# Moving the two halves of an output bank together: two half-bank copies and two adds, or one whole-bank copy and two adds across partitions

## The chip, the cores and the metric

The program runs on one core of a Trainium2 chip. The core has a matrix engine (TensorE, PE), a vector engine (VectorE, DVE), a scalar engine (ScalarE, ACT), a general engine (GpSimd, POOL) and a queue engine that issues most transfers (SyncE, SP). Each engine takes its instructions in the order in which they stand in its own queue, and waits on semaphores for the others. SBUF and PSUM are memories of 128 partitions; PSUM has banks of 512 float32 per partition. The metric is the device time of one launch in microseconds; less is better.

## The reference

A two-layer decoder trunk over 1024 tokens of width 1024, 16 heads of 64 in 4 key/value groups. Layer 0 has a native sparse attention (attention A in this document), layer 1 a dilated attention (attention B). Each is followed by an output projection and a SwiGLU feed-forward block. Cut to what matters here:

```python
# layer 0: three branches, gated and summed per head
o = g[..., 0:1] * o_cmp + g[..., 1:2] * o_sel + g[..., 2:3] * o_win
# layer 1: three (window, dilation) groups, merged by their softmax denominators
alpha = jax.nn.softmax(jnp.stack(lses, axis=-1), axis=-1)
o = jnp.einsum('bsgrdi,bsgri->bsgrd', jnp.stack(outs, axis=-1), alpha)
# in every branch: o = softmax(q k^T * scale + bias, masked) v
```

The product of the probabilities with v is what the change touches: how it leaves PSUM.

## The kernel before

Values are float32 throughout. Where a product needs more than one pass of the matrix engine, an operand is split into a rounded high part and the rest: `v` is stored with the high part in columns 0 to 63 and the low part in columns 64 to 127. A product of `v` with probabilities, both parts of `v` at once, therefore gives 128 partitions: partitions 0 to 63 (the lower half) hold the share of the high part and partitions 64 to 127 (the upper half) that of the low part. The two must be added across partitions, once per output bank. That is `evac_o` (L353 to L360).

An output bank `o` (PSUM, 128 x 512) holds the four heads of one group for 128 tokens, 128 columns per head. In `ov` the heads are numbered by c (0, 1) and e (0, 1). Heads with e = 0 go to the lower half of `dst`, heads with e = 1 to the upper half. For each e, `own` is the half that the result is written to and `oth` the other one: ScalarE copies the other half of the bank to the partitions of `own` in the SBUF buffer `ot` (L359), and VectorE adds the bank's own half and the copy (L360). There are two `o` banks (BANKS, L30).

Attention A (L624 to L866) runs over 4 groups g and 8 tiles t of 128 tokens. For each (g, t) come a compressed-block job (`cmp_job`), which opens the bank with L760 and L761, and four `dense_job`s: window branch and selected-block branch, each for two pairs of heads (hp). A job does scores on PE (L790, L791), bias and minimum on VectorE (L793), exponentials on ScalarE (L799), normalising on GpSimd (L803). Its `back` part transposes the probabilities on PE (L328), moves them to SBUF as `th` (ScalarE, L165) and `tl` (VectorE, L166), or by a plain copy `traw` (L332, L340), and multiplies with `v` (L347 to L349). The last `back` of a (g, t) calls `evac_o`, which writes to `oT`.

Attention B (L1560 to L1783) has for each of 4 groups 8 wide jobs per head pair (`wide_job`, dilation groups 1 and 2 together, result to `o12`, whose tokens lie 8 apart) and then 8 near jobs per head pair (`near_job`, dilation group 0, result to `oTb`). Scores, bias (L1641), exponentials (L1646) and the `back` part follow the same pattern. The second head pair of each pair calls `evac_o`. A generator `merge` joins the results of a group (L1702 to L1747). So `evac_o` runs 32 times in A, 32 times for wide and 32 times for near jobs.

`pipelined` puts the `back` part of a job two jobs later. Beyond that the order is not written by hand: the tile framework's scheduler decides, from its own estimate of durations, in which order instructions stand in each engine's queue (`schedule_with_timeline_sim`, L1835). So an edit in `evac_o` can move other instructions too. After each attention comes `out_proj` (L1219), whose first loads are `ow` (L1228, weights) and `xr` (L1237, the residual stream).

Of the kernel before, what the change touches and what calls it, by code (L numbers as in the profile page):

```python
# [10 lines left out]
F32 = mybir.dt.float32  # L11
F32R = mybir.dt.float32r
BF = mybir.dt.bfloat16
AF = mybir.ActivationFunctionType
# [101 lines left out]
def trunk(ctx, tc, I, out):  # L116
    nc = tc.nc
# [235 lines left out]
    def evac_o(p, po, dst):  # L353

        ov = po[:].rearrange("p (c e q) -> p c e q", e=2, q=128)
        tmp = p.tile([128, 2, 128], F32, name="ot", bufs=2)
        for e in range(2):
            own, oth = slice(64 * e, 64 * e + 64), slice(64 - 64 * e, 128 - 64 * e)
            nc.scalar.activation(tmp[own], ov[oth, :, e, :], AF.Copy)  # L359
            nc.vector.tensor_add(dst[own], ov[own, :, e, :], tmp[own])  # L360

    def pipelined(jobs, lag=1):

# [260 lines left out]
    with ExitStack() as c:  # L624
# [139 lines left out]
        def dense_job(g, t, br, hp):  # L764
# [41 lines left out]
            def back():  # L806
                po = po_[g, t]
                for b0 in range(0, nb, 2):
                    bs = range(b0, min(b0 + 2, nb))
                    th, tl = transposed(wk, [P[:, e, b * 128:(b + 1) * 128] for b in bs for e in range(2)],  # L810
                                        (cp_a, cp_v)[hp] if br == 2 and b0 == 2 else None,
                                        whole=br == 2 and hp == 1 and b0 == 0)
                    for i, b in enumerate(bs):
                        last = br == 1 and b == nb - 1
                        cs = slice(i * 256, (i + 1) * 256)
                        o_ = po[:, hp * 256:(hp + 1) * 256]
                        v_ = grp["V", br - 1, g, (k0 + b) // 4][:, (k0 + b) % 4, :]
                        mm_pv(o_, v_, th, tl, cs, False, last)
                if br == 1 and hp == 1:
                    evac_o(wk, po, oT[:, 2 * g:2 * g + 2, tok(t)])  # L820
# [739 lines left out]
    with ExitStack() as c:  # L1560
# [73 lines left out]
        def unit(key, hp, stats, slot, score, bias, n, blocks, dst):  # L1634
# [14 lines left out]
            def back():  # L1649
                if hp == 0:  # L1650
                    po_[key] = bank("o"), None
                po, prev = po_[key]
                nb = len(blocks)
                for b0 in range(0, nb, 2):
                    bs = range(b0, min(b0 + 2, nb))
                    th, tl = transposed(wk, [P[:, e, b * 128:(b + 1) * 128] for b in bs for e in range(2)],
                                        pick(hp, b0, nb), 5, unsplit(key, hp))
                    for i, b in enumerate(bs):
                        cs = slice(i * 256, (i + 1) * 256)
                        o_ = po[:, hp * 256:(hp + 1) * 256]  # L1660
                        with after(prev if b == 0 else None):
                            prev = mm_pv(o_, blocks[b], th, tl, cs, b == 0, b == nb - 1)
                po_[key] = po, prev
                if hp == 1:
                    evac_o(wk, po, dst)
# [173 lines left out]
```

## Time and profile before

| | us |
|---|---|
| median of 3 runs | 2975.21 |
| lowest and highest run | 2972.13, 2981.29 |
| span of the profiled execution, first to last instruction | 2969.9 |

For the profiled execution no time is given beside its span; the median of the runs, which also holds what lies around the span, is 5.3 us above it. The page gives busy time for each engine. For VectorE and ScalarE an instruction's time is what it keeps the engine; on PE the ends of matmuls are modelled and neighbours overlap, so a busy PE is not PE at its peak. The name after the line number is the tile that is written, then what is read. The granted TensorE clock is 0.989 on average and 1.00 in both attentions.

### The profile page before, as it was taken

The page shows a single profiled execution, that of the slowest core. Times are in us where ns is not written, and L with a number is a line of the kernel's source. Part 1 is how long each engine was busy: PE and PEld are TensorE (multiplying, and loading weights), DVE is VectorE, ACT ScalarE, POOL GpSimd, SP SyncE. Part 2 cuts the span into 40 slices and gives each one's busy share as a digit, 9 for nine tenths or more (in the row PEclk, how much of TensorE's full clock was granted, in tenths as well). Part 3 has the DMA queues.
Part 4 walks back from the last instruction along what each step waited for, and adds up shares of the span by engine and source line. Part 5 has one row for each costly group of instructions (what it writes and reads, how often), then busy time and mean ns, then how long its engine had stood idle before and what let it go on. Part 6 is the DMA issues. An engine that isn't in the chain of part 4 may idle for free.

```text
span 2969.9 us, 44462 instructions
## 1 busy us (share of the span) xinstructions
PE 2839.8 (96%) x14734; PEld 2368.8 (80%) x14734; DVE 2398.1 (81%) x4875; ACT 1608.9 (54%) x3614; POOL 1607.7 (54%) x1718
## 2 busy tenths in 40 slices
PE   9999999999999999999999999899989999999997
PEld 8888888887777788788777788788867787887885
DVE  5553988988888888988876676699998888888887
ACT  5432888897553333333454444799965433333334
POOL 3135766764565555555557786444426655556551
PEclk9999999999999999999999999999999999999998
DMA  8678133113222222231224555966340211112112
GB/s 252 209 246 285 46 91 87 54 30 118 68 62 64 73 75 62 62 81 53 86 81 143 160 165 152 288 195 181 101 167 22 68 57 53 57 47 64 54 43 75
DMA packets 277318, 317.58 MB, mean 107 GB/s; under 512 B 19196, under 2 KB 210733, under 8 KB 277088
## 3 DMA queue, kind: packets, MB, share of 16 engines
q1 hardware_dynamic: 255344, 246.50, 27.9%
q0 software_dynamic: 21744, 68.23, 7.1%
q8 instruction: 117, 1.92, 0.3%
q14 instruction: 113, 0.93, 0.1%
HBM read 243.17 MB, written 87.20 MB: 111 GB/s over the span
## 4 chain that ended last, share of the span: by engine, by line
PE 62%; DVE 23%; ACT 6%; issue 4%; POOL 2%; DMA 2%; SPq 1%; DVEq 0%; ACTq 0%; POOLq 0%
PE ux L203 5%; PE ux L204 5%; DVE pl L885 5%; PE ux L205 5%; PE uy L203 4%; PE uy L204 4%; PE uy L205 4%; DVE xr L943 4%; PE dx L204 3%; PE dx L205 3%; PE pt L328 3%; PE dr L203 3%; PE dx L203 3%; PE mm L204 3%; PE mm L203 3%
## 5 line engine op out<-in xcount | busy, mean ns | idle before, releaser
L885 DVE TENSOR_TENSOR pl<-oT,ph 128x512 fp32r<-128x512 f32 x319 | 327.2, 1045 | 42.5 <-ACT ph L884 37.2
L884 ACT ACTIVATE ph<-oT 128x512 fp32r<-128x512 f32 x329 | 198.4, 625 | 206.8 <-PE ux L204 58.9
L328 PE MATMUL pt<-ident,P 128*128 128x128 f32 x1536 | 242.3, 275 | 10.6 <-DVE tl L166 4.9
L885 DVE TENSOR_TENSOR pl<-oTb,ph 128x512 fp32r<-128x512 f32 x233 | 222.3, 979 | 25.2 <-ACT ph L884 25.2
L166 DVE TENSOR_TENSOR tl<-pt,th 128x512 fp32r<-128x512 f32 (+1 forms) x336 | 217.4, 652 | 26.8 <-ACT th L165 25.5
L884 ACT ACTIVATE ph<-oTb 128x512 fp32r<-128x512 f32 x239 | 142.8, 625 | 170.2 <-PE ux L204 52.5
L943 DVE TENSOR_TENSOR xr<-xr,dr 128x512 f32<-128x512 f32 x320 | 204.3, 678 | 29.9 <-PE dr L205 29.9
L204 PE MATMUL dx<-pl,ph 128*128 128x512 f32 x512 | 206.3, 403 | 9.9 <-DVE pl L885 7.3
L803 POOL TENSOR_SCALAR P<-P,sm,gates 128x384 f32<-128x384 f32 (+7 forms) x256 | 182.5, 724 | 45.2 <-DVE sm L801 40.0
L165 ACT ACTIVATE th<-pt 128x512 fp32r<-128x512 f32 (+1 forms) x336 | 185.0, 564 | 37.4 <-PE pt L328 31.6
L205 PE MATMUL dx<-ph,pl 128*128 128x512 f32 x512 | 202.5, 398 | 0.3 <-DVE pl L885 0.3
L328 PEld LDWEIGHTS pt<-ident,P 128*128 128x128 f32 x1536 | 177.7, 141 | 31.4 <-DVE tl L166 5.2
L943 DVE TENSOR_TENSOR xr<-xr,dx 128x512 f32<-128x512 f32 x320 | 199.9, 676 | 2.5 <-PE dx L205 1.8
L203 PE MATMUL dx<-ph 128*128 128x512 f32 x512 | 165.6, 403 | 15.9 <-DVE nss L1016 7.9
L799 ACT ACTIVATE P<-P,m 128x384 f32<-128x384 f32 (+7 forms) x256 | 170.6, 669 | 9.0 <-DVE m L797 7.2
L1269 POOL TENSOR_TENSOR oT<-oT,gffn 128x512 f32<-128x512 f32 x92 | 107.7, 1177 | 118.8 <-DMA oT<-in_ffn_w_up_dram 96.5
L348 PE MATMUL o<-th,V 128*128 128x256 f32 x572 | 158.7, 297 | 4.5 <-DVE o L360 1.7
L349 PE MATMUL o<-tl,V 128*128 128x256 f32 x572 | 158.2, 299 | 4.7 <-DVE tl L166 1.7
L1269 POOL TENSOR_TENSOR oTb<-oTb,gffn 128x512 f32<-128x512 f32 x92 | 106.5, 1167 | 87.9 <-DMA oTb<-in_ffn_w_up_dram 79.8
L341 POOL TENSOR_SCALAR th<-traw 128x256 fp32r<-128x256 f32 x112 | 95.4, 852 | 98.2 <-ACT traw L340 33.1
L1646 ACT ACTIVATE P<-P,st 128x384 f32<-128x384 f32 (+2 forms) x256 | 139.9, 548 | 6.3 <-DVE st L1641 5.0
L203 PEld LDWEIGHTS dx<-ph 128*128 128x128 f32 x512 | 97.8, 191 | 45.4 <-ACT nss L1015 8.7
(629 smaller groups left out, 9487.8 us busy)
## 6 DMA issues: line engine op xcount, KB each, us to landing
qB<-xr POOLq DMA_DIRECT2D x96, 256.0 KB, 4.6
oT<-in_ffn_w_up_dram SPq DMA_DIRECT2D x92, 256.0 KB, 3.0
oTb<-in_ffn_w_up_dram SPq DMA_DIRECT2D x92, 256.0 KB, 3.0
Q<-qB SPq DMA_DIRECT2D x40, 512.0 KB, 6.4
wd<-in_ffn_w_down_dram SPq DMA_DIRECT2D x66, 256.0 KB, 2.6
oT<-in_b_w_q_dram SPq DMA_DIRECT2D x48, 256.0 KB, 3.4
K<-kBs SPq DMA_DIRECT2D x40, 256.0 KB, 9.6
wraw<-in_a_w_in_dram SPq DMA_DIRECT2D x18, 512.0 KB, 7.1
```

The lines of the kernel that those rows point to most:

```text
L165: prev = nc.scalar.activation(H_, src, AF.Copy)
L166: rest = (eng or nc.vector).tensor_sub(L_, src, f32(H_))
L203: nc.tensor.matmul(ps, lh, rh, start=first, stop=False, skip_group_check=bool(shared))
L204: nc.tensor.matmul(ps, lh, rl, start=False, stop=False, skip_group_check=bool(shared))
L205: return nc.tensor.matmul(ps, ll, rh, start=False, stop=last, skip_group_check=bool(shared))
L328: nc.tensor.transpose(ps[:, i * 128:(i + 1) * 128], b, ident)
L799: nc.scalar.activation(P[:, e, :n], P[:, e, :n], AF.Exp, bias=mm[:, e:e + 1], scale=-1.0, accum_out=sm[:, e:e + 1])
L803: nc.gpsimd.tensor_scalar(P[:, e, :n], P[:, e, :n], sm[:, e:e + 1], gt(g, t, br, 2 * hp + e, 1), op0=OP.mult, op1=OP.mult)
L884: nc.scalar.activation(h, src, AF.Copy)
L885: (eng or nc.vector).tensor_sub(l, src, f32(h))
L943: nc.vector.tensor_add(xs, xs, banks[t])
L1269: nc.gpsimd.tensor_mul(v, v, gains[:, k:k + 4].unsqueeze(2).to_broadcast([128, 4, 128]))
```

## The change

The buffer `ot` gets the size of a whole bank (128 x 2 x 2 x 128 in place of 128 x 2 x 128) and one place instead of two, so it takes the same memory. ScalarE copies the whole bank to it once, every partition to itself. VectorE then does its two adds: for each e, the own half of the bank, read from PSUM, and the other half of the copy, read from SBUF at the other partitions. Until now both inputs and the output of an add lay on the same partitions.

```diff
     def evac_o(p, po, dst):
 
         ov = po[:].rearrange("p (c e q) -> p c e q", e=2, q=128)
-        tmp = p.tile([128, 2, 128], F32, name="ot", bufs=2)
+        tmp = p.tile([128, 2, 2, 128], F32, name="ot", bufs=1)
+        nc.scalar.copy(tmp[:].rearrange("p c e q -> p (c e q)"), po)
         for e in range(2):
             own, oth = slice(64 * e, 64 * e + 64), slice(64 - 64 * e, 128 - 64 * e)
-            nc.scalar.activation(tmp[own], ov[oth, :, e, :], AF.Copy)
-            nc.vector.tensor_add(dst[own], ov[own, :, e, :], tmp[own])
+            nc.vector.tensor_add(dst[own], ov[own, :, e, :], tmp[oth, :, e, :])
```

ScalarE has 192 half copies (64 x 256) before and 96 copies (128 x 512) after; every other engine has the same instructions, in another order inside the two attentions. Outside of them only the start of the output projection after A, with its loads, has changed order.

First place: VectorE in attention B, wide jobs of the second group, near their end. Before (`ot` is the buffer, `o_21047` the result `o12`, `st_21045` the row statistics, `T_...` the bias; what a row waits for is in brackets):

```order
L166 TENSOR_TENSOR tl<-pt,th 128x512 [waits Activation_49]
L360 TENSOR_TENSOR o_21047<-o,ot 64x256 [waits Activation_49]
L1641 ISA P,st_21045<-s,T_20684 128x384 [waits PE_49]
L1641 ISA st_21045 128x1
L360 TENSOR_TENSOR o_21047<-o,ot 64x256 [waits Activation_49]
L1641 ISA P,st_21045<-s,T_20687 128x384 [waits PE_49]
L1641 ISA st_21045 128x1
L166 TENSOR_TENSOR tl<-pt,th 128x512 [waits Activation_49]
```

Each of the two adds of a bank waits for ScalarE, and other work stands between them. The same place on VectorE after the change (`o_21000` is `o12`, `st_20998` the statistics):

```order
L166 TENSOR_TENSOR tl<-pt,th 128x512 [waits Activation_49]
L360 TENSOR_TENSOR o_21000<-o,ot 64x256 [waits Activation_49]
L360 TENSOR_TENSOR o_21000<-o,ot 64x256
L1641 ISA P,st_20998<-s,T_20643 128x384 [waits PE_49]
L1641 ISA st_20998 128x1
L1641 ISA P,st_20998<-s,T_20646 128x384 [waits PE_49]
L1641 ISA st_20998 128x1
L166 TENSOR_TENSOR tl<-pt,th 128x512 [waits Activation_49]
```

The two adds stand next to each other and only the first waits; this is so for all 96 banks.

Second place: ScalarE in attention B, near jobs of the second group. Before:

```order
L359 ACTIVATE ot<-o 64x256 [waits PE_49,Activation_49]
L165 ACTIVATE th<-pt 128x512 [waits PE_49]
L359 ACTIVATE ot<-o 64x256 [waits DVE_49]
L1646 ACTIVATE P,st_21046<-P,st_21046 128x256 [waits DVE_49] x2
L165 ACTIVATE th<-pt 128x512 [waits PE_49]
L1728 ACTIVATE cc<-cc 128x32 [waits DVE_49]
L332 COPY traw<-pt 128x512 [waits PE_49,Pool_49]
L1646 ACTIVATE P,st_21046<-P,st_21046 128x256 [waits DVE_49,Activation_49]
L359 ACTIVATE ot<-o 64x256 [waits DVE_49]
```

The first copy of a bank waits for PE, the second for VectorE, which has the first add to do before. The same place on ScalarE after the change:

```order
L332 COPY traw<-pt 128x512 [waits PE_49,Pool_49]
L1646 ACTIVATE P,st_20999<-P,st_20999 128x256 [waits DVE_49]
L357 COPY ot<-o 128x512 [waits DVE_49,PE_49,Activation_49]
L1728 ACTIVATE cc<-cc 128x32 [waits DVE_49]
L165 ACTIVATE th<-pt 128x512 [waits PE_49]
L1646 ACTIVATE P,st_20999<-P,st_20999 128x256 [waits DVE_49] x2
L165 ACTIVATE th<-pt 128x512 [waits PE_49]
L1646 ACTIVATE P,st_20999<-P,st_20999 128x256 [waits DVE_49] x3
L357 COPY ot<-o 128x512 [waits DVE_49,PE_49,Activation_49]
```

One copy per bank is left. It waits for PE's last product into the bank and, since `ot` has one place, in some rows for VectorE's adds of the bank before.

Third place: SP's queue behind attention A, the first loads of `out_proj`. Before:

```order
L1228 DMA ow<-in_a_w_out_dram 128x512 x8
L1228 DMA ow<-wS_81 128x512
L1237 DMA xr<-in_x_dram 128x1024 x4
L1228 DMA ow<-wS_81 128x512 x3
L1237 DMA xr<-in_x_dram 128x1024 x4
```

And SP's queue at the same place after the change:

```order
L1228 DMA ow<-in_a_w_out_dram 128x512 x5
L1237 DMA xr<-in_x_dram 128x1024 x4
L1228 DMA ow<-in_a_w_out_dram 128x512 x3
L1228 DMA ow<-wS_81 128x512 x4
L1237 DMA xr<-in_x_dram 128x1024 x4
```

Three of the eight `ow` loads, and one of `wS`, have moved behind the first four `xr` loads.

## The prediction

> **What bounds the kernel now.** On the page I look at the slices (each a fortieth of 2969.9 us) of the two engines that the change uses.
>
> ```profile
> span 2969.9 us, 44462 instructions
> ...
> DVE  5553988988888888988876676699998888888887
> ACT  5432888897553333333454444799965433333334
> ```
>
> ScalarE (ACT) is much busier in slices 4 to 9 and 25 to 29 than elsewhere: the two attentions, the only callers of `evac_o`. So I asked for busy times by stretch. The columns are the stretch, its length, busy us and counts of PE, PEld, DVE, ACT, POOL, then clock and DMA. First stand attention A and attention B, then a sum over near jobs of B, then three stretches of its wide jobs.
>
> ```profile
> 295.00:730.00 435.00, 412.25 (x2854) 366.84 (x2854) 387.73 (x1537) 375.75 (x1084) 288.64 (x466) 1.00 0.21 61
> ...
> 1890.00:2200.00 310.00, 289.09 (x2124) 255.90 (x2122) 286.97 (x891) 283.79 (x820) 126.36 (x158) 1.00 0.56 169
> ...
> sum 118.00, PE 106.18 PEld 91.56 DVE 108.40 ACT 115.80 POOL 10.60; mean PE 21.24 PEld 18.31 DVE 21.68 ACT 23.16 POOL 2.12
> ...
> 1966.00:2006.00 40.00, 39.05 (x305) 35.68 (x304) 37.71 (x110) 35.91 (x104) 27.77 (x35) 1.00 0.55 155
> ...
> 2036.00:2078.00 42.00, 41.19 (x318) 37.83 (x316) 40.60 (x116) 37.81 (x109) 29.09 (x36) 1.00 0.44 141
> ...
> 2110.00:2152.00 42.00, 40.74 (x318) 37.62 (x318) 40.66 (x113) 37.32 (x106) 27.89 (x33) 1.00 0.05 14
> ```
>
> The sum is of five stretches: 1905 to 1920 (still wide, before the first near jobs), 1932 to 1962, 2010 to 2034, 2080 to 2107 and 2158 to 2180. In them ACT works 115.8 of 118 us: the near jobs are **bound by ScalarE**, with VectorE (DVE) at 108.4 close behind. In the three wide stretches DVE works 119.0 of 124 us (37.71 + 40.60 + 40.66), ACT 111.0. PE's figures are as high there, but its matmuls overlap and their ends are modelled, so I take the wide jobs as **bound by VectorE**. In A the bound moves about; I looked at one head group, 452 to 562 us, in stretches of 10 us and added those where one engine leads:
>
> ```profile
> sum 30.00, PE 27.20 PEld 23.04 DVE 28.25 ACT 29.36 POOL 24.85; mean PE 13.60 PEld 11.52 DVE 14.13 ACT 14.68 POOL 12.42
> ...
> sum 40.00, PE 37.49 PEld 33.43 DVE 38.64 ACT 32.98 POOL 27.98; mean PE 18.74 PEld 16.71 DVE 19.32 ACT 16.49 POOL 13.99
> ```
>
> The first sum is 452 to 462 and 522 to 542, where ACT leads (29.36 of 30). The second is 462 to 472 and 532 to 562, where DVE is over 95% (532 to 542 is in both). In the rest PE leads or nobody does.
>
> **The copies.** The rows of the buffer `ot`, and the row of the one full-bank copy by the same engine that exists already, `traw`:
>
> ```profile
> L359 ACT ACTIVATE ot<-o x192: 375/380/385, 298.9 to 2192.7; 64x256 f32<-64x256 f32 x192
> L360 DVE TENSOR_TENSOR o<-o,ot x64: 602/644/689, 1893.4 to 2165.9; 64x256 f32<-64x256 f32 x64
> L360 DVE TENSOR_TENSOR oTb<-o,ot x64: 406/422/429, 1936.3 to 2193.3; 64x256 f32<-64x256 f32 x64
> ...
> L332 ACT COPY traw<-pt 128x512 f32<-128x512 f32 x40 | 23.1, 578 | 2.2 <-PE pt L328 2.0
> ```
>
> There are 96 banks: 32 in A, 32 wide and 32 near ones in B. Two copies of 380 ns become one, which I price as `traw`'s 578 ns: ACT saves 0.18 us a bank, 17 us in all. That counts only where ACT leads. In the same stretches, `ot`'s own busy times are:
>
> ```profile
> sum 118.00, DVE 22.46 ACT 17.44; mean DVE 4.49 ACT 3.49
> ...
> sum 30.00, DVE 2.50 ACT 2.27; mean DVE 1.25 ACT 1.13
> ```
>
> 17.44 us are 46 copies, 23 banks: 23 x 0.18 = 4.1 us. DVE then stands just as high (108.4 plus what the next part adds, against 115.8 - 4.1 = 111.7), so I count half, **-2.1 us**. In A 2.27 us are 6 copies, 3 banks a head group: 4 x 3 x 0.18 = **-2.1 us**.
>
> **The adds.** Their number stays, 192, but now they stand back to back (first order table above), and the bank's half and the copy's half lie on different partitions. What that costs is in the gaps between DVE instructions. The rows are start, us, engine, line; first two wide adds with their neighbours, then two near ones:
>
> ```profile
> 2047.77 0.66 DVE L360 TENSOR_TENSOR o<-o,ot 64x256 f32<-64x256 f32 x1
> 2048.25 0.70 DVE L1746 TENSOR_TENSOR o<-o,pt 128x512 f32<-128x512 f32 x1
> ...
> 2050.74 0.09 DVE L1641 DVE_READ_ACCUMULATOR2_ANT st<- 128x1 f32 x1
> 2050.86 0.69 DVE L360 TENSOR_TENSOR o<-o,ot 64x256 f32<-64x256 f32 x1
> 2051.58 0.56 DVE L1641 CUSTOM_DVE_ANT_0 P<-s,T 128x384 f32<-128x384 f32 x1
> ```
>
> ```profile
> 2088.33 0.09 DVE L1641 DVE_READ_ACCUMULATOR2_ANT st<- 128x1 f32 x1
> 2088.33 0.41 DVE L360 TENSOR_TENSOR oTb<-o,ot 64x256 f32<-64x256 f32 x1
> 2088.67 0.41 DVE L1641 CUSTOM_DVE_ANT_0 P<-s,T 128x256 f32<-128x256 f32 x1
> ...
> 2092.18 0.08 DVE L1641 DVE_READ_ACCUMULATOR2_ANT st<- 128x1 f32 x1
> 2092.29 0.43 DVE L360 TENSOR_TENSOR oTb<-o,ot 64x256 f32<-64x256 f32 x1
> 2092.75 0.25 DVE L1732 RECIPROCAL mx<-mx 128x16 f32<-128x16 f32 x1
> ```
>
> The first of each two is a lower-half add (e = 0, all operands from partition 0): it starts 0.09 before the instruction ahead ends, and the next starts before it ends, by 0.07 (near) or 0.18 (wide, 2048.43 against 2048.25). The second is an upper-half add (e = 1, all from partition 64): 0.03 free before it, 0.03 behind, no overlap. So entering or leaving the upper half costs an overlap. Before, a bank has the gaps -0.09, -0.07 (wide -0.18), +0.03 and +0.03: -0.10 near, -0.21 wide. After, if the lower-half add, whose copy half now starts at partition 64, is held as well, there are three gaps of +0.03, and two neighbours that the second add stood between now overlap by 0.09: 0.00. That is **+0.10 us a bank near, +0.21 wide**. No row shows an add whose operands lie in different halves. If it isn't held on entry, the sum is 0.12 lower: about 0 near, +0.09 wide. I take the upper values, since the nearest row, the upper-half add, reads that operand at the same partitions. The add itself could also be dearer or cheaper; the copies below, half of which move between halves, bound that within 10 ns (685 to 695 for the 512-element form), so I take nothing.
>
> ```profile
> L410 DVE COPY kc<-mm x12: 417/685/695, 32.8 to 139.9; 64x512 f32<-64x512 f32 x8, 64x256 f32<-64x256 f32 x4
> ```
>
> [...]
>
> On the bound: the last three of four wide parts, 24 banks x 0.21 = **+5.0 us** (the first, 1890 to 1932, waits for loads); in A, DVE leads in 40 of 110 us, 32 x 0.10 x 40/110 = **+1.2 us**.
>
> **The waits.** Until now a bank went copy, add, copy, add, since the second copy waits for the first add. Rows of waits, in B (who for whom, us, times, longest), and of the adds in the whole kernel:
>
> ```profile
> ACT ot L359 <- DVE oTb L360: 2.5, 5, 0.8
> ...
> PE o L348 <- DVE o L360: 1.7, 6, 0.8
> ```
>
> ```profile
>   ACT ot L359: 5.9, 13
> ```
>
> The first goes: **-2.5 us**, on the engine that leads there. It could be replaced: with one buffer for `ot` the copy now waits for the adds of the bank before. Behind it in ACT's queue stand the exponentials and `th`, for which DVE and PE wait. I price that at nothing, since banks come every 4 us or more and two adds take 0.9 (near) or 1.3. The second row is PE's wait for a free `o` bank; it is freed sooner, but PE doesn't lead, so nothing. The last is DVE's idle time before adds, in 13 of 192; a copy 0.2 longer makes it at most 13 x 0.2 = 2.6 worse, and half as many waits make it better: nothing.
>
> **Loads after A.** In the third order table four `xr` loads stand ahead of three `ow` loads on SP's queue.
>
> ```profile
> 710.71 4.26 SPq L1228 DMA_DIRECT2D ow<-in_a_w_out_dram  x8
> ...
> 725.01 1.75 SPq L1237 DMA_DIRECT2D xr<-in_x_dram  x4
> ```
>
> ```profile
> ow<-in_a_w_out_dram SPq DMA_DIRECT2D x12, 256.0 KB, 6.1
> ```
>
> ```profile
> 732.72 1.14 ACT L884 ACTIVATE ph<-ow 128x512 fp32r<-128x512 f32 x2
> ```
>
> `xr` waits until 725.01, so the three go out from 726.8 and land 6.1 later, 732.9, up to 735 if `xr`'s 2 MB are ahead of them. ACT wants the first at 733.3 (second of the two). Between 0 and 2 us: **+1.0**.
>
> Sum: -2.1 - 2.1 + 5.0 + 1.2 - 2.5 + 1.0 = **+0.5 us** on a span of 2969.9. The runs shown have a median of 2975.2, 5.3 above it; I add the sum there: **2975.7**.
>
> **The rivals.** *Faster:* the holds fall into time in which DVE would wait anyway. For it speaks that DVE has 10 us free in 118 near, against it only 5 in 124 wide. Then ACT's relief counts in full: -4.1 - 2.1 - 2.5, and PE's wait -1.7: -10.4, **2964.8**. With all 17 us of ACT's saving on the path it ends at 2954. *Slower:* DVE becomes the bound throughout. Every hold is on the path: A and near 64 x 0.10, wide 32 x 0.21, together 13.1 us, the longer wait for a full copy 2.6, and ACT's relief buys nothing: **2990.9**. It decides from the point where DVE is over 95% busy in near jobs and in most of A: then two thirds of the 13.1 are the 8.9 us that I call slower. For it speaks DVE's 92% in near jobs; against it that PE or ACT leads in much of A. *It doesn't do what it says:* the scheduler could have kept the adds apart; the order shows them adjacent, so no chance is left for that. The scheduler also set the other instructions of both attentions anew; nothing in the trace prices that, and it widens both sides.
>
> **How the numbers follow.** A measurement of this kernel tells 0.3%, 8.9 us, from no change. The forecast, gain and loss about equal, has 0.44 and ends within 0.3%; the faster rival 0.27, the slower one 0.29. Each rival's price passes 8.9 us, so these are the three chances too. The forecast's own range is 2967 to 2984. For 8 in 10 I go to the slower rival's time, 2991, and down past the faster one's, to 2959.
>
> **What would show it.** Right: `ot` x96 near 0.58 us; ACT's share in near jobs down from 98% to about 95%; adds back to back with 0.03 us ahead of, between and behind them; A and B within 5 us of 435 and 310. Wrong: the lower-half add overlapping what is ahead of it (then faster), a copy over 0.65 us, DVE idle before adds clearly above 5.9 us, or FFN stages that move.

## The result, and the profile after

| | before | after |
|---|---|---|
| median, us | 2973.67 (2963.49 to 2981.29, 6 runs) | 2995.91 (2990.66 to 3000.28, 6 runs) |
| ratio | 1 | 1.0069, 95% interval 1.0055 to 1.0084 |
| span of the profiled execution, us | 2969.9 | 2996.9 |

The change makes the kernel slower by 0.7%. (The quotient of the two medians is 1.0075; the text goes by the ratio in the table, 1.0069.) The time lies 4.9 us above the range that was predicted. First the page of the kernel after: its span and the slices of VectorE and ScalarE.

```profile
span 2996.9 us, 44364 instructions
...
DVE  5443988988888988888876676689998888888887
ACT  5432887887553333333454444678865533333334
```

ScalarE has become lighter where it was heaviest, in slices 4 to 9 and 25 to 29. Busy times of attention A and attention B after (stretch, length, busy us and counts of PE, PEld, DVE, ACT, POOL, then clock and DMA):

```profile
295.00:745.00 450.00, 422.88 (x2871) 370.47 (x2869) 394.13 (x1549) 364.41 (x1064) 289.37 (x470) 0.99 0.20 56
1905.00:2225.00 320.00, 290.26 (x2114) 259.56 (x2115) 286.92 (x885) 257.68 (x751) 122.64 (x156) 0.98 0.57 167
```

ScalarE's work fell from 375.75 to 364.41 us in A and from 283.79 to 257.68 in B, and yet the stretches that hold A and B are 15 and 10 us longer. VectorE's share of A did not rise (394.13 of 450 is 88%, before 387.73 of 435, 89%). The rows of `ot` after (ns least, median, most; start of the first and the last):

```profile
L357 ACT COPY ot<-o x96: 557/574/632, 300.9 to 2222.7; 128x512 f32<-128x512 f32 x96
L360 DVE TENSOR_TENSOR oT<-o,ot x64: 416/422/429, 302.3 to 741.9; 64x256 f32<-64x256 f32 x64
L360 DVE TENSOR_TENSOR o<-o,ot x64: 615/650/692, 1914.2 to 2190.0; 64x256 f32<-64x256 f32 x64
L360 DVE TENSOR_TENSOR oTb<-o,ot x64: 416/422/429, 1956.6 to 2223.9; 64x256 f32<-64x256 f32 x64
```

The copy costs what was priced (574 ns), the add no more than before within 10 ns (650 ns against 644 in the wide jobs, 422 against 422 and 423 elsewhere). From the first to the last add, A now takes 439.6 us (302.3 to 741.9; before 300.1 to 727.6, 427.5) and B 309.7 (1914.2 to 2223.9; before 1893.4 to 2193.3, 299.9).

For the table of all runs below, A is counted from the start of its first score product to that of the output projection's first product, B from its first score product to its last add, both read off the timeline. By that count A went from 446.2 to 459.6 and B from 319.5 to 329.1. The feed-forward stage between them went from 1147.3 to 1152.8, but it also reads 1144.6 and 1154.6 in kernels whose order there is the same, so a difference of 10 us there, between two single executions, means nothing; the whole is judged by the ratios.

### The profile page after: what moved, and what is told of

It is laid out like the page before. It is cut to its first block, busy times and chain, and to the rows that moved or that the text cites. A ratio compares the mean times of both kernels' runs of the same rounds, so it can differ in the third digit from the quotient of the medians.

```text
span 2996.9 us, 44364 instructions
## 1 busy us (share of the span) xinstructions
PE 2850.1 (95%) x14734; PEld 2373.4 (79%) x14734; DVE 2409.7 (80%) x4875; ACT 1573.5 (53%) x3518; POOL 1611.2 (54%) x1718
## 5 line engine op out<-in xcount | busy, mean ns | idle before, releaser
L799 ACT ACTIVATE P<-P,m 128x384 f32<-128x384 f32 (+7 forms) x256 | 172.1, 679 | 17.5 <-DVE m L797 11.9
L349 PE MATMUL o<-tl,V 128*128 128x256 f32 x572 | 164.6, 309 | 7.5 <-DVE tl L166 5.4
```

The lines of the kernel that those rows point to most:

```text
L799: nc.scalar.activation(P[:, e, :n], P[:, e, :n], AF.Exp, bias=mm[:, e:e + 1], scale=-1.0, accum_out=sm[:, e:e + 1])
```

## The experiments

Two theories stood at the start. **Holds:** the adds that cross partitions no longer overlap their neighbours, and VectorE pays. **Order:** the scheduler, given other durations, drew another order for everything in both attentions, and that order is worse. A third came up on the way: the **bank** `o` is given free at another moment.

| run | what it is | ratio, 95% interval | A, us | B, us |
|---|---|---|---|---|
| before | | 1 | 446.2 | 319.5 |
| after | | 1.0069, 1.0055 to 1.0084 | 459.6 | 329.1 |
| e1 | old copies left on their partitions | 1.0027, 1.0016 to 1.0038 | 446.7 | 327.7 |
| e2 | after, adds on one half | 1.0044, 1.0028 to 1.0060 | 457.2 | 321.8 |
| e3 | new evacuation in A alone | 1.0063, 1.0042 to 1.0084 | 461.6 | 322.1 |
| e4 | new evacuation in B alone | 1.0011, 1.0000 to 1.0023 | 445.5 | 325.0 |
| e5 | both half copies, then both adds | 1.0087, 1.0070 to 1.0104 | 469.4 | 326.4 |
| e6 | after, and a 2-column copy between the adds | 1.0131, 1.0111 to 1.0151 | 468.7 | 345.9 |
| e7 | after, and a 128-column copy between the adds | 1.0140, 1.0116 to 1.0165 | 473.6 | 347.7 |
| e8 | after, the copy in two column halves | 1.0060, 1.0042 to 1.0077 | 463.4 | 325.6 |
| e9 | after, in the order of before | 1.0007, 0.9997 to 1.0016 | 446.5 | 322.6 |
| e10 | half copies, in the order of after | 1.0084, 1.0070 to 1.0098 | 469.9 | 325.3 |
| e11 | A alone, in the order of before | 1.0007, 0.9994 to 1.0019 | 447.0 | 320.8 |
| e12 | the same, adds apart | 0.9987, 0.9976 to 0.9998 | 445.1 | 319.9 |

### The adds alone, in the old order

```diff
-            nc.scalar.activation(tmp[own], ov[oth, :, e, :], AF.Copy)
-            nc.vector.tensor_add(dst[own], ov[own, :, e, :], tmp[own])
+            nc.scalar.activation(tmp[oth], ov[oth, :, e, :], AF.Copy)
+            nc.vector.tensor_add(dst[own], ov[own, :, e, :], tmp[oth])
```

> The kernel of before with one edit: each half copy stays on its own partitions and the add reads it from there, so the add has its two inputs in different halves as after the change. Every engine's queue has the same order as before and ScalarE has the same 192 copies. Holds theory (VectorE loses the overlap around the lower-half add, and that is the loss): the lower-half add is held on entry and exit, 0.21 us a bank in A and near, 0.31 wide, 64 x 0.21 + 32 x 0.31 = 23 us of VectorE time, of which 12 to 23 us end in the time. Order theory (the new order of the queues is the loss, the holds fall into idle time): 0 to 6 us slower than before.

Every engine keeps before's order; only the partitions of the copy change, so that each add crosses. The kernel is 0.27% slower, about 8 us: between the figures of the two theories (0 to 6 and 12 to 23). A stays (446.7), B becomes 8.2 us longer. So holds cost something in B, nothing that shows in A, and they leave A's 13 us unexplained.

### The order alone, without the held entry

```diff
-            nc.vector.tensor_add(dst[own], ov[own, :, e, :], tmp[oth, :, e, :])
+            nc.vector.tensor_add(dst[own], ov[own, :, e, :], tmp[own, :, e, :])
```

> The changed kernel with one edit: both inputs of an add are read from the same half, so what is added is not the two parts of the product (the output is not the reference's). Every engine's queue has the same order as after the change; only the hold on entry of the lower-half add is gone, 96 x 0.11 = 11 us of VectorE time. Holds theory: 7 to 11 us faster than the changed kernel, so 10 to 14 us slower than before. Order theory: within 4 us of the changed kernel, 16 to 24 us slower than before.

This is the kernel after, in its own order, but with both inputs of an add on the same partitions; it leaves out the sum of the two parts. Its time is 0.25% below that of after, about 7 us (the intervals overlap a little). That is the figure of the holds theory (7 to 11 us), not that of the order theory (at most 4). By stages it looks otherwise: B comes back to 321.8, A stays long at 457.2. Most of A's loss does not hang on the crossing, but in this order the crossing costs B about 7 us.

### One attention at a time

```diff
                 if hp == 1:
-                    evac_o(wk, po, dst)
+                    evac_o2(wk, po, dst)
             return back
```

> The new evacuation in attention A alone, the old one in B. From the profiles A grew by 13 us and B by 9 between the two kernels. If each stage's loss is its own: 9 to 15 us slower than before, all of it between the first and the last instruction of A. If the loss in A is an accident of this one schedule and of the profiled execution: under 5 us.

> The old evacuation in attention A, the new one in B. If each stage's loss is its own: 6 to 11 us slower than before, all of it in B. Holds theory alone: B has 64 banks, 32 x 0.10 + 32 x 0.21 = 10 us of VectorE time, A 3 us, so B's share of the loss would be three quarters, 15 us; order theory says nothing on the split.

`evac_o2` is the other form of the evacuation; in e3 B keeps the old one, in e4 A does. A alone gives 0.63%, 19 us, more than the 9 to 15 expected; B alone gives 0.11%, 3 us, less than the 6 to 11, though both intervals reach into those figures. Most of the loss belongs to A. The attention that is named here has changed in order too: A has the order of after in e3 and that of before in e4, while B has an order of its own in both.

### Other evacuations, each in the order that it draws

```diff
-            nc.scalar.activation(tmp[own], ov[oth, :, e, :], AF.Copy)
-            nc.vector.tensor_add(dst[own], ov[own, :, e, :], tmp[own])
+            nc.scalar.activation(tmp[own], ov[oth, :, e, :], AF.Copy)
+        for e in range(2):
+            own, oth = half(e)
+            nc.vector.tensor_add(dst[own], ov[own, :, e, :], tmp[own])
```

> The kernel of before with both half copies written ahead of both adds. ScalarE keeps its 192 half copies, no add has its inputs in different halves, the bank is free early, and the scheduler gives attention A a third order, unlike that of before and that of the changed kernel. Where A (first compressed score to first product of the output projection) took 446 us before and 460 after. Theory 'lucky draw' (the order of before is an unusually good one, and any evacuation that makes the scheduler draw again loses): A 452 to 462 us, 6 to 18 us slower than before. Theory 'early bank' (an early free bank and adjacent adds lead the scheduler to bad orders): the same here. Holds theory: A 445 to 448, no slower than before.

Here no add crosses partitions, and A is 469.4, longer than after the change and than the 452 to 462 expected. Holds are out as the cause in A.

```diff
+            if e == 1:
+                nc.scalar.activation(tmp[oth, 1, 1, 126:128], ov[oth, 1, 1, 126:128], AF.Copy)
             nc.vector.tensor_add(dst[own], ov[own, :, e, :], tmp[oth, :, e, :])
```

> The changed kernel with a copy of two columns by ScalarE between the two adds, so that a bank goes copy, add, copy, add again and is freed late, as before. The order of A is a fourth one. Lucky draw: A 452 to 462 us. Early bank: A 445 to 450 us. The added copies are 96 x 0.2 us of ScalarE time, as much as the change saves.

> As the run before, but the copy between the adds has 128 columns, a quarter of the bank's data. A fifth order. Lucky draw: A 452 to 462 us. Early bank: A 445 to 450 us. ScalarE has 0.1 us a bank more than before the change, so B up to 6 us slower than with the changed kernel's ScalarE time.

Both put the wait of ScalarE for the first add back (e7 copies 128 columns instead of 2) and so hold the bank for longer. A did not come back, 468.7 and 473.6, and so the theory of the bank falls. Both lie above the figures of the other theory too. B became far worse (345.9 and 347.7), much more than the 6 us allowed for in e7; why was not looked into.

```diff
-        nc.scalar.copy(tmp[:].rearrange("p c e q -> p (c e q)"), po)
+        for c in range(2):
+            nc.scalar.copy(tmp[:, c].rearrange("p e q -> p (e q)"), po[:, c * 256:(c + 1) * 256])
```

> The changed kernel with its copy cut in two by columns (two of 128 x 256, about 0.73 us together, as much as the half copies of before); bank free early, adds adjacent, inputs in different halves. Another order of A. Lucky draw and early bank: A 452 to 462 us. In B the hold costs as in the changed kernel, and ScalarE's relief is gone: B at least as long as the changed kernel's 329 us if the relief was worth anything.

A 463.4, a little above its figures, B 325.6, the time that of after within the intervals. B is below the 329 us of after, so ScalarE's relief shows no worth there, though B's order differs as well. Every kernel that drew A anew has A between 457 and 474, whatever its evacuation, a wider spread than the 452 to 462 that was expected; the three that kept before's order or code there (before, e1, e4) have 445 to 447. That points to the order, but doesn't show it yet.

### The order as the only variable

The last four runs hold every engine's queue to a given order. All instructions are written as before; then, for each engine, every instruction is tied behind the one that should stand ahead of it (an order of issue, no wait). Shortened; in the kernels the loop stands in a function of its own, and the lists are packed into a text:

```diff
     with tile.TileContext(nc, schedule_with_timeline_sim=True) as tc:
         trunk(tc, aps, o)
+        for q in queues:            # one list of instruction numbers for each engine
+            for a, b in zip(q, q[1:]):
+                tc.add_manual_dep(traced[b], traced[a].name, no_sync, reason="issue_after")
```

> The whole change (one copy of the bank, two adds across partitions, one place for the buffer), but every engine's queue is held to the order of the kernel before; PE, GpSimd and SyncE have exactly its rows, ScalarE's copy stands where the first half copy stood, and the two adds stand together where the first add stood. Order theory (A lengthens because the scheduler drew another order): A is again 444 to 449 us (before 446.2, after 459.6), B 323 to 329 for the holds (before 319.5, after 329.1), the time 3 to 9 us above before. Evacuation theory (A lengthens because of the copy and the adds themselves, whatever the order): A 455 to 460, the time 15 us or more above before.

> The other way round: two half copies and two adds on their own partitions, as before the change (both copies ahead of both adds), but every queue is held to the order of the kernel after; VectorE, PE, GpSimd and SyncE have exactly its rows, and the two half copies stand where the whole copy stood. No add crosses partitions. Order theory: A 455 to 462 us and B 318 to 325, the time 8 to 15 us above before. Evacuation theory: A 444 to 449, the time within 4 us of before. With its own drawn order the same evacuation had A at 469.4.

With these two there is a table of two by two (A, B, ratio):

| | order of before | order of after |
|---|---|---|
| half copies, adds on their own partitions | 446.2, 319.5, 1 (before) | 469.9, 325.3, 1.0084 (e10) |
| whole copy, adds across partitions | 446.5, 322.6, 1.0007 (e9) | 459.6, 329.1, 1.0069 (after) |

Read by rows, the order costs 0.8% with the old evacuation and 0.6% with the new one. Read by columns, the new evacuation costs 0.07% in the old order (interval -0.03 to 0.16), and in the new order it is no dearer than half copies. (e10 has both copies ahead of both adds, where the whole copy stood; with its own drawn order the same code is e5. So its 0.8% is the order and the place of the second copy together; copies first in the order of before was not run. The pairs that differ in order alone are e9 and after, and e11 and e3.) The order theory's figures for e9 hold for A; B and the time came out a little below them. In e10, A and the time (0.84%, 25 us) lie above its figures, on the side that the evacuation theory excludes. **The order is shown to be the cause** of A's lengthening and of most of the loss, by e9 against after and, below, e11 against e3. The adds' rows of e9 say the same of A, 426.4 us from first to last (before 427.5, after 439.6):

```profile
L357 ACT COPY ot<-o x96: 557/578/641, 300.3 to 2196.8; 128x512 f32<-128x512 f32 x96
L360 DVE TENSOR_TENSOR oT<-o,ot x64: 416/423/430, 301.7 to 728.1; 64x256 f32<-64x256 f32 x64
```

> The new evacuation in attention A alone, the old one in B, and every queue held to the order of the kernel before; in A the two adds stand together where the first stood. With its own drawn order this was 20 us slower than before, with A at 461.6. Order theory: A 443 to 448, B and the rest as before, the time within 3 us of before, perhaps 1 or 2 below it since ScalarE saves 6 us in A. Evacuation theory: A 455 to 460, the time 9 us or more above before.

> As the run before this one, but the two adds of a bank in A stand apart, each where it stood before the change, so VectorE, PE, GpSimd and SyncE all have exactly the rows of before and only ScalarE's copies are fewer. It shows what the place of the second add is worth: the bank is given free later than with the adds together, but the second add can wait for nothing. Order theory: A 443 to 448, within 2 us of the run with the adds together. Evacuation theory: A 455 to 460.

Between e3 and e11 only the order differs: 1.0063 becomes 1.0007, and A 447.0, as the order theory had it. With the two adds apart, at the places that they had, it is the fastest kernel of this study: 2974.23 us against 2977.73 of before on that chip, ratio 0.9987 (0.9976 to 0.9998). That is below the 0.3% that the prediction calls a difference, though its interval leaves out 1. The step from e11 to e12 is larger than the 2 us expected of the second add's place, but their intervals overlap.

### What the new order does in A

The same wait in the four kernels of the table, for A's stretch, in the order before, after, e9, e10 (who for whom: us in total, times, longest): PE at its product with the high part, for GpSimd, which makes that part.

```profile
PE o L348 <- POOL th L341: 0.7, 1, 0.7
```

```profile
PE o L348 <- POOL th L341: 5.8, 5, 2.3
```

```profile
PE o L348 <- POOL th L341: 1.7, 3, 1.2
```

```profile
PE o L348 <- POOL th L341: 7.8, 4, 2.7
```

This row goes with the order, not with the evacuation. It is no sum, though: PE's wait for the other part, which the same engine makes, went the other way. Before and after:

```profile
PE o L349 <- POOL tl L342: 4.9, 7, 1.6
```

```profile
PE o L349 <- POOL tl L342: 1.7, 4, 0.7
```

One case on the timeline of after (start, us, engine, line; in brackets idle time and releaser):

```profile
382.33 1.00 PE L713 MATMUL s<-kc,Q 128*128 128x64 f32 x8
...
383.05 0.23 POOL L670 COPY C<-T 128x32 f32<-128x32 f32 x1 [2.14 <-DMA T<-sA]
...
384.29 0.23 POOL L672 COPY C<-T 128x31 f32<-128x31 f32 x1 [1.01 <-DMA T<-sA]
...
384.50 0.85 POOL L341 TENSOR_SCALAR th<-traw 128x256 fp32r<-128x256 f32 x1
...
385.40 0.39 PE L348 MATMUL o<-th,VW 128*128 128x256 f32 x1 [2.07 <-POOL th L341]
```

GpSimd has the `th` behind copies that wait for a transfer, PE has that product ahead of everything else, and so the transfer stops PE for 2.07 us. In the order of before, PE has other score products there; its stop at this place is half of that, before and in e9 (6 us earlier before has one of 1.57, for `tl`):

```profile
384.19 0.39 PE L349 MATMUL o<-tl,VW 128*128 128x256 f32 x1 [1.06 <-POOL tl L342]
```

```profile
385.63 0.39 PE L349 MATMUL o<-tl,VW 128*128 128x256 f32 x1 [1.08 <-POOL tl L342]
```

Behind this stop the clock falls as well. After, by the microsecond (PE busy, then the granted clock):

```profile
385.00:386.00 1.00, 0.60 (x4) 0.92 0.94 229
386.00:387.00 1.00, 1.00 (x7) 0.50 1.00 227
387.00:388.00 1.00, 1.00 (x6) 0.50 1.14 283
388.00:389.00 1.00, 1.00 (x6) 0.50 0.98 229
389.00:390.00 1.00, 1.00 (x10) 0.88 0.58 160
```

Counted as time at 0.50, the five clocks give 3.4 us (0.16 + 3 + 0.24). e10, with the old evacuation and the same order, stops at the same place, and its clock falls there too, by the same count for 3.4 us (0.76 + 2 + 0.66):

```profile
385.94 0.39 PE L348 MATMUL o<-th,VW 128*128 128x256 f32 x1 [1.97 <-POOL th L341]
```

```profile
386.00:387.00 1.00, 1.00 (x6) 0.62 1.03 227
387.00:388.00 1.00, 1.00 (x6) 0.50 1.06 209
388.00:389.00 1.00, 1.00 (x6) 0.50 1.06 223
389.00:390.00 1.00, 1.00 (x8) 0.67 1.00 201
```

The slices of A with a clock below 1.00, after:

```profile
380.00:400.00 20.00, 17.93 (x133) 0.91 0.50 131
580.00:600.00 20.00, 17.86 (x99) 0.94 0.27 67
600.00:620.00 20.00, 17.03 (x127) 0.98 0.44 119
```

They lose 20 x (0.09 + 0.06 + 0.02) = 3.4 us of clock. Before, e1, e4, e9, e11 and e12 have no such slice in A; all eight kernels whose A is in another order have some, and lose between 3.4 us (after) and 17 us (e7). This is the clearest sign of the new orders, but it is only a part of A's 13.4 us, and the other 10 can't be placed. PE's wait for `th` has grown by 5.1 us (5.8 - 0.7), yet PE's idle time as a whole does not tell the orders apart. Stretch of A before, after and in e9 (length, then PE's busy time first):

```profile
282.00:727.00 445.00, 421.17 (x2921) 374.66 (x2921) 394.12 (x1601) 385.03 (x1132) 296.12 (x484) 1.00 0.22 63
```

```profile
284.00:742.00 458.00, 429.81 (x2920) 376.63 (x2920) 398.49 (x1599) 371.16 (x1099) 295.28 (x484) 0.99 0.21 59
```

```profile
283.00:728.00 445.00, 417.93 (x2923) 374.51 (x2922) 390.14 (x1598) 371.83 (x1099) 295.54 (x484) 1.00 0.23 63
```

PE is idle for 23.8 us before, 28.2 after and 27.1 in e9, where A is not longer. What is longer after than in e9 is the time in which PE counts as busy with the same products, 11.9 us; a busy PE in this profile is not PE at its peak. ScalarE's wait for PE's transposes, after and in e9, is no clear sign either, since it is long in e9 too:

```profile
ACT th L165 <- PE pt L328: 43.8, 55, 2.9
```

```profile
ACT th L165 <- PE pt L328: 35.2, 54, 2.1
```

Whether taking away the stops, or any other wait, would bring A back was not tried.

## Why the prediction was wrong, and where it was right

**The step that failed** is the last sentence on the rivals, that the scheduler had set the other instructions of both attentions anew, that nothing prices it and that it widens both sides. It got no term in the sum, and the range had no room for a loss of 18 us. The ratios of after and e9, 1.0069 / 1.0007, put it at 0.62%, 18 us, nearly all of the loss. The order tables showed VectorE, ScalarE and SyncE around the change; PE's queue, which has no instruction of the change in it and was drawn anew all the same, was not looked at. How the new order takes the time is shown only in part (the clock in A). Nor do order and instructions simply add: in the old order the whole new evacuation costs 2 us, in the new one the crossing alone about 7 (e2).

**The sum of the other terms, +0.5 us, agrees with e9**, but in part by luck, since single terms were off in both directions. e9 is the change without the new order: 0.07% of 2974 is 2 us, with an interval of -1 to +5. By its terms:

- *Copy, 0.58 us for two of 0.38:* right, 574 ns and 578.
- *Holds:* right that the lower-half add, with its inputs in different halves, no longer overlaps, and right in the size of the gaps. Ahead of the lower-half add after the change, where an overlap of 0.09 had been, 0.03 are free, and 0.02 behind the pair (VectorE, wide jobs):

```profile
2107.86 0.42 DVE L1641 CUSTOM_DVE_ANT_0 P<-s,T 128x256 f32<-128x256 f32 x1
2108.20 0.09 DVE L1641 DVE_READ_ACCUMULATOR2_ANT st<- 128x1 f32 x1
2108.32 1.28 DVE L360 TENSOR_TENSOR o<-o,ot 64x256 f32<-64x256 f32 x2
2109.62 0.42 DVE L1641 CUSTOM_DVE_ANT_0 P<-s,T 128x256 f32<-128x256 f32 x1
```

  2108.20 + 0.09 to 2108.32 is 0.03; 1.28 for two adds of about 0.64 leaves next to nothing between them, where 0.03 had been taken.
- *In A* the holds cost nothing that shows (e1: 0.5 us against the 1.2 counted), and ScalarE's relief, counted at -2.1, shows nothing in e9 (+0.3). With the adds left apart, in e12, A is 1.1 us shorter than before.
- *In B* the terms were -2.1 + 5.0 - 2.5 = +0.4; e9 shows +3.1. The gaps of the holds are there; if they cost their 5.0, the gains were 1.9 in place of 4.6, but e9 does not separate the two. In the near stretches of e9, 3 us later than before (4 in the last), ScalarE works 110.52 of 118 us and VectorE 111.62: VectorE stands a little ahead now, for which half of the relief had been cut. The other half is not seen either: the exponentials' wait for VectorE grew from 5.0 us in B before (first row) to 18.1 in e9 (second), by more than the 64 x 0.18 = 11.5 us that ScalarE saves in B:

```profile
sum 118.00, PE 107.46 PEld 92.77 DVE 111.62 ACT 110.52 POOL 12.16; mean PE 21.49 PEld 18.55 DVE 22.32 ACT 22.10 POOL 2.43
```

```profile
ACT P L1646 <- DVE st L1641: 5.0, 11, 0.9
```

```profile
ACT P L1646 <- DVE st L1641: 18.1, 30, 1.3
```

- *The vanished wait, -2.5:* after the change ScalarE's copy waits for the adds of the bank before, on the one place of `ot`, for longer than it had waited inside a bank. This was priced at nothing, since banks come 4 us or more apart. It too belongs to the new order: in e9 it is 0.9 us, once. The row is that of after:

```profile
ACT ot L357 <- DVE oTb L360: 3.6, 5, 1.4
```

- *Loads after A, +1.0:* they cost nothing. (The upper end of its landing time, 735, was set too early: at the 422 GB/s that the profile of before has from 728 to 729, the 2 MB of `xr` take 5 us.) PE's first product there waits 1.7 us for ScalarE after, 2.0 before, and no wait for a transfer stands in those rows.

**The rivals.** The slower rival's time, 2990.9, came near by chance, not by its mechanism: VectorE's share of A fell. The test that the prediction set itself, A and B within 5 us, is what gave it away: A is 13 off, B 10.

## What to carry to other kernels

Where a scheduler sets the queues, an edit is two changes: the instructions, and a new order for everything near them. Price them apart, by running the new instructions in the old order and the old instructions in the new order; here the first was 0.07%, and the order 0.6% (with the new instructions) to 0.8% (with the old ones). And read the order of the engine that is busiest in that stage, not only of those whose instructions the diff touches.

## What the runs showed of the hardware that was not expected

Stops of PE of 2.07 us (after) and 1.97 us (e10) were each followed by 3.4 us at a granted clock of 0.50 (above), but in these runs the length of a stop does not decide it. In after, a stop of 1.20 us, with one of 0.24 behind it, was followed by the second fall, at 597.5 (clock 0.73 from 597 to 598, then 0.50); the longest one, 2.26 us before 615.42, left the clock at 1.00:

```profile
595.45 0.39 PE L348 MATMUL o<-th,VW 128*128 128x256 f32 x1 [1.20 <-POOL th L341]
```

```profile
615.42 0.39 PE L348 MATMUL o<-th,VW 128*128 128x256 f32 x1 [2.26 <-POOL th L341]
```

```profile
615.00:616.00 1.00, 0.58 (x5) 1.00 0.03 8
616.00:617.00 1.00, 1.00 (x12) 1.00 0.00 0
```

In e3 the clock fell at 471.5 although none of PE's stops in the 10 us before was longer than 0.4 us:

```profile
PE pt L328 <- ACT QM L763: 0.4, 1, 0.4
```

```profile
471.00:472.00 1.00, 0.69 (x2) 0.73 0.00 0
472.00:473.00 1.00, 1.00 (x5) 0.50 0.00 0
```

What makes the clock fall, these runs don't show.

ScalarE's copies have a fixed part: 2 columns of 64 partitions took 165 ns (e6), 128 took 271 (e7), against 380 for 256 before the change. From these three I estimate 163 ns and 0.85 ns for each column; for 512 columns that gives 598, and the whole-bank copy took 574.

```profile
L361 ACT ACTIVATE ot<-o x96: 144/165/211, 305.6 to 2247.2; 64x2 f32<-64x2 f32 x96
```

```profile
L361 ACT ACTIVATE ot<-o x96: 250/271/317, 307.0 to 2259.0; 64x128 f32<-64x128 f32 x96
```
